# Twelve modulation units of a transformer kernel computed on TensorE instead of seven, five of them at changes between stages

## The chip, the cores and the metric

The kernel runs on one core of a Trainium2 chip. The metric is the device time of one execution in microseconds (us); the number given for a kernel is the median of its runs. TensorE is called PE in the rows (its weight loads PEld), VectorE is DVE, ScalarE is ACT, GpSimd is POOL, and SyncE, which issues the DMAs, is SP.

## The reference, cut to what matters

Two transformer blocks of two layers each run one after the other on 256 tokens of width 1024, in float32. The second block is modulated: each of its layers computes, from a condition vector, six rows of 1024 numbers (shift, scale and gate for the mixer, and the same for the feed-forward part), once for the latent tokens and once for 256 context tokens.

```python
for l in range(DEPTH):                               # second block, DEPTH = 2
    mod_l = jnp.split((silu(c) @ ada_w[l] + ada_b[l])[:, None, :], 6, axis=-1)
    mod_c = jnp.split((silu(c_ctx) @ ada_w[l] + ada_b[l])[None, None, :], 6, axis=-1)
    hl = modulate(x_lat, norm_g[l, 0], mod_l[0], mod_l[1])     # rms_norm * (1 + scale) + shift
    hc = modulate(x_ctx, norm_g[l, 0], mod_c[0], mod_c[1])
    ...                                              # even or odd mixer
    x_lat = x_lat + mod_l[2] * (mix_l @ w_out[l])
    x_lat = x_lat + mod_l[5] * conv_ffn(modulate(x_lat, norm_g[l, 1], mod_l[3], mod_l[4]), ...)
    ...                                              # the same for x_ctx with mod_c, in layer 0
```

The change concerns how `mod_l` and `mod_c` are computed and when. The first block does not use them.

## The kernel before

**Stages.** One program goes through the stages a0 (first attention mixer), f0 (its feed-forward part), a1, f1 (first block, layer 1), even (the even mixer of the second block), f2 (its feed-forward part), odd (the odd mixer) and f3. Each stage is a list of steps, a step being a list of weight keys and a function that emits instructions. `weave(a, b)` (L307) spreads the steps of b evenly between those of a.

**Weights.** All big matrices are streamed from HBM as units of up to 128 x 1056 numbers, in the order in which the steps name them. `fetch` (L481) issues the DMA of a unit into `raw` and splits it: ACT rounds it into `wh` (L496), DVE subtracts to get the rest `wl` (L497). Before a step that uses unit n is emitted, the units up to n + 4 are fetched (`UNITS_AHEAD`, L38). `raw`, `wh` and `wl` have four buffers each (L39 to L42), so unit n + 4 can only be split when unit n has been used up. A full product is three matmuls: high by high, high by low, low by high.

**Order.** The framework keeps the program order as a priority and orders each engine's instructions itself, taking the first whose inputs and buffers it expects to be free. The resulting order of each engine is fixed in the program.

**PSUM.** Accumulators come from pools: three banks `acc`, two `s`, two `t`, one `o` (L870). Output projections (`p_out`, L625), the gate half of a feed-forward part and the modulation units on PE all take an `acc` bank.

**Modulation.** The 6 x 1024 columns of one layer are 24 units of 256 columns; the two layers make units 0 to 47. `ada_upto` (L567) issues the units in order from a running counter `ada_at`. `ada(slot)` (L561) moves the counter on by the number that the table `ADA` (L317) holds for this slot. `ada_need(l, n)` moves it to where a coming stage needs it. There are two ways to compute a unit:
- on DVE: two blocks of 128 columns. Each loads 128 x 1024 numbers (`adaw`, 512 KB, from SP) and runs one multiply-and-reduce (L591) for each condition. Units 0 to 31 take two per block, units 32 to 47 one, as the context is not needed then.
- on PE (`p_ada`, L599), for the units in `ADA_PE` (L40): two weight units of 512 rows x 256 columns, which go through the `raw`, `wh`, `wl` ring like any other, 8 matmuls of 256 columns for each of them with the split condition `csil` as the stationary side, one copy to `adarow` on ACT (L616), four small matmuls that turn the rows, and one addition on DVE.

Before, `ADA_PE` is 13 to 19, and all seven lie in the middle of the even mixer (slots "e.0", "e.1", "e.2", with 3, 2 and 2 units), woven among the mLSTM heads' projections.

**Changes of stage.** `plan_attn0` and `plan_attn1` end with `p_out` of the last quarter of the mixer's rows, and the feed-forward part begins with gate and up products of `nh`, `nl`. The even mixer begins with `even_norm` (L1203): statistics, then `modulate` (L1134, per 128 channels one DVE `nt` L1143, one ACT `nh` L1145, one DVE `nl` L1146) over eight channel groups, interleaved with a scaling of x (L1216). f2 ends with the down products of the latents, while the context is already modulated for the odd mixer; the odd mixer's first products (`p_nout` of "kv" and "k", L531) are of the context.

Of the kernel before, what the change touches and what calls it, by code (L numbers as in the profile page):

```python
# [17 lines left out]
S = 256  # L18
# [18 lines left out]

UNITS_AHEAD = 4  # L38
RAW_BUFS = 4  # L39
ADA_PE = range(13, 20)  # L40
HI_BUFS = 4
LO_BUFS = 4  # L42
CUTS = 1
# [4 lines left out]
def _ar(a, n):  # L48
    return np.arange(a, a + n)
# [6 lines left out]
def unit_specs():  # L56
# [3 lines left out]
    def add(key, w, l, rows, cols):  # L60
        assert key not in u
        u[key] = (w, l, rows, cols)

    def halves(key, w, l, cols):
        for kh in range(2):
            add(key + (kh,), w, l, _ar(512 * kh, 512), cols)
# [11 lines left out]
                add(key + ("d", m, t), down, l, _ar(128 * j0, 128 * (j1 - j0)), _ar(128 * m, 128))  # L78

    for i in ADA_PE:  # L80
        halves(("ada", 0, i), "ada_w_2", 0, _ar(256 * i, 256))
    for g in range(2):
        for j, n in enumerate("qkv"):
            halves(("a", n, g), "hyb_w_in", 0, _ar(512 * j + 256 * g, 256))
# [222 lines left out]
def weave(a, b, tail=0):  # L307
    out, n, i = [], max(len(b) - tail, 0), 0
    for k, s in enumerate(a):
        out.append(s)  # L310
        while i < n and i * len(a) < (k + 1) * n:
            out.append(b[i])
            i += 1
    return out + b[i:]


ADA = {  # L317
    "a0.0": 0, "a0.1": 1, "a0.2": 1, "a0.3": 2, "f0": 1, "f1": 4, "e.0": 3, "e.1": 2, "e.2": 2, "f2": 28,
}


# [55 lines left out]
class Prog:  # L377
    def __init__(self):
        self.specs = unit_specs()
        self.ada_at = 0  # L380
        self.steps = self.plan()
        self.order = []
        seen = set()
        for keys, _ in self.steps:
            for k in keys:
                if k not in seen:
                    seen.add(k)
                    self.order.append(k)
        self.utab = unit_table(self.order, self.specs)
# [177 lines left out]
    def ada_upto(self, n, room=True):  # L567
# [3 lines left out]
        for i in range(a, self.ada_at):  # L571
            if i in ADA_PE:
                out += self.p_ada(i // 24, i % 24)
# [331 lines left out]
    def plan_attn0(self):  # L905
# [22 lines left out]
        def proj_a(g):  # L928
            b = boxes[g]
            return (self.p_rope(("a", "q", g), b, "q", -0.125) + self.p_rope(("a", "k", g), b, "k", None)  # L930
                    + self.p_v(("a", "v", g), b))
# [55 lines left out]
        out = self.p_open("0", first) + proj_a(0)  # L987
# [3 lines left out]
        out += weave(attend(boxes[3], "mask_c", 3, ext(1)),  # L991
                     self.ada("a0.3") + self.p_out(("o0", 0), 128, self.mixes(0, 6), S, self.x_add()))
        out += self.ada("a0.t")
        out += self.p_out(("o0", 1), 512, self.mixes(6, 8), S, self.x_add((self.st0,), "fn0"))
        return out + self.p_close()

    def plan_ffn1(self, l, st, nst, fill, gn=None, mid=(), side=()):
# [46 lines left out]
    def plan_attn1(self, st, fill, early):  # L1044
# [18 lines left out]
        def proj(g):  # L1063
            b = boxes[g]
            return (self.p_rope(("d", "q", g), b, "q", -0.125) + self.p_rope(("d", "k", g), b, "k", None)
                    + self.p_v(("d", "v", g), b))
# [51 lines left out]
        out = self.p_open("1", first) + fill + proj(0)  # L1118
# [1 line left out]
            out += weave(attend(g), proj(g + 1) + early("a1.%d" % g) + self.ada("a1.%d" % g))  # L1120
        out += weave(attend(3), early("a1.3") + self.ada("a1.3") + self.p_out(("o1", 0), 128, self.mixes(0, 6), S, self.x_add()))
        out += early("a1.t") + self.ada("a1.t")
        out += self.p_out(("o1", 1), 512, self.mixes(6, 8), S, self.x_add((self.st1,), "fn1"))
        return out + self.p_close()

    def scales(self, l, w):
# [136 lines left out]
    def plan_even(self, s1, s2):  # L1263
# [69 lines left out]
        def pairs(ts, i0, i1):  # L1333
            return Lazy(lambda: [(ts[i][0][:, p], ts[i][1][:, p]) for i in range(i0, i1) for p in range(2)])
# [201 lines left out]
        o_l = [self.p_out(("o2", "l%d" % i), 512, pairs(E.sl, i, i + 1), S, xm(LAT, *st[1:2 * i])) for i in range(2)]  # L1536
# [5 lines left out]
        def early(slot):  # L1542
            out = []
            for n, at in EC.items():
                if at == slot:
                    if n == "kvg":
                        out += [((), setup)] + kvg(0)
                    elif n == "g":
                        out += gprep(0)
                    elif n == "oc":  # L1550
                        out += self.ada_need(0, 12) + o_c
                    elif n[0] == "q":
                        out += proj_q(int(n[1]), False)
                    elif slot == "f1":
                        out += attend(int(n[1]), False)
            return out
# [7 lines left out]
        out = self.p_open("2", first) + early("e.a") + self.ada("e.a")  # L1564
# [25 lines left out]
        for k in slots:  # L1590
# [2 lines left out]
            out += weave(chain[k], fill[k], EV["tail"] if k in "b0123" else 0)  # L1593
            if k in "b012":
                out += decay(slots.index(k))
        out += o_l[1]
        yield out + self.p_close() + [((), lambda: self.evctx.close())] + self.plan_ffn2a(st[1])

    def plan_ffn2a(self, sl):
# [3 lines left out]
        out = self.p_open("f2")  # L1603
# [25 lines left out]
        for t, (j0, j1) in enumerate(THIRDS):  # L1629
# [8 lines left out]
            if t == 0:  # L1638
# [7 lines left out]
                n0 = len(out)  # L1646
# [20 lines left out]
                if i == 0:  # L1667
                    out.append(((), lambda: self.modulate(1, 0, st[0])))
        self.st_odd = st[1]
        return out[:n0] + weave(out[n0:], self.ada("f2")) + self.p_close()  # L1670

    def plan_ffn2b(self, st):
        l, key, W = 1, ("f3",), S + 2
# [224 lines left out]
```

## Time and profile before

| | us |
|---|---|
| median of 3 runs (lowest, highest) | 1726.1 (1724.31, 1729.87) |
| the profiled execution | 1726.9 |
| its span, first to last instruction | 1725.1 |
| PE busy in the span | 1670.7 (97%) |
| DVE busy | 1371.5 (80%) |
| ACT busy | 945.7 (55%) |

The profiled execution's own time is 1.8 us above its span and 0.8 us above the median. A matmul's recorded length overlaps its successor, so the distance from start to start tells what one costs in a stream. The granted clock of PE is given as a share of 2.4 GHz; the two levels are 2.4 and 1.2 GHz, and a value between them is a mean over the stretch.

### The profile page before, as it was taken

What the parts mean: (1) busy time and instruction counts of PE and PEld (TensorE: products, weight loads), DVE (VectorE), ACT (ScalarE), POOL (GpSimd) and SP (SyncE); (2) the same over time, 40 slices, a digit from 0 to 9 for tenths busy, and PEclk for the clock granted to TensorE, in tenths of its full rate; (3) what the DMA queues carried; (4) which work ended last, traced back from release to release, by engine and by line L of the source; (5) the groups of instructions that cost most, each with busy time, mean ns of one, the idle gap of its engine ahead of it and who ended that gap; (6) DMA issues with size and microseconds to landing.
All of it is one profiled execution on the core that took longest, in us unless ns stands there. A gap on an engine that the chain in (4) does not pass through costs nothing.

```text
span 1725.1 us, 31957 instructions
## 1 busy us (share of the span) xinstructions
PE 1670.7 (97%) x12336; PEld 1574.1 (91%) x12336; DVE 1371.5 (80%) x2830; ACT 945.7 (55%) x1687; POOL 59.0 (3%) x75
## 2 busy tenths in 40 slices
PE   7999999999899999999989999999998999999999
PEld 7999999999899999899978988888888998999999
DVE  6798999887787888766786888897779864479887
ACT  6666456656675768444545652342344554466554
POOL 0000000000100000100000000000000220000000
PEclk9999999999999999999989999999998999799999
DMA  8446776554456565334311555655549521135663
GB/s 305 140 142 220 231 219 210 173 173 132 125 173 194 184 206 162 123 124 133 110 62 41 181 182 165 189 169 185 181 150 315 184 62 38 62 121 165 198 191 123
DMA packets 80664, 277.97 MB, mean 161 GB/s; under 512 B 8960, under 2 KB 12160, under 8 KB 80256
## 3 DMA queue, kind: packets, MB, share of 16 engines
q1 hardware_dynamic: 79216, 273.30, 49.6%
q10 hardware_dynamic: 1296, 2.62, 0.4%
q8 instruction: 97, 1.59, 0.4%
q14 instruction: 55, 0.45, 0.1%
HBM read 274.84 MB, written 1.05 MB: 160 GB/s over the span
## 4 chain that ended last, share of the span: by engine, by line
PE 83%; DVE 10%; ACT 4%; issue 2%; DMA 0%; POOL 0%; DVEq 0%; ACTq 0%; POOLq 0%
PE acc L501 55%; PE s L501 20%; PE o L501 4%; DVE wl L497 3%; DVE junk L591 2%; PE ptp L820 2%; ACT wh L496 1%; PE tt L741 1%; DVE x L856 0%; DVE cc L1025 0%; PE stv L501 0%; PE tt L836 0%; DVE nt L1143 0%; ACT L1373 0%; DVE stq L691 0%
## 5 line engine op out<-in xcount | busy, mean ns | idle before, releaser
L496 ACT ACTIVATE wh<-raw 128x1024 fp32r<-128x1024 f32 (+4 forms) x446 | 453.7, 1025 | 453.5 <-PE acc L501 323.6
L497 DVE TENSOR_TENSOR wl<-raw,wh 128x1024 fp32r<-128x1024 f32 (+4 forms) x446 | 524.1, 1180 | 115.1 <-ACT wh L496 113.1
L501 PE MATMUL acc<-nh,wh 128*128 128x256 f32 (+2 forms) x872 | 269.0, 309 | 3.0 <-ACT nh L1145 1.9
L501 PE MATMUL acc<-nh,wl 128*128 128x256 f32 (+2 forms) x872 | 268.7, 308 | 0.5 <-DVE wl L497 0.3
L501 PE MATMUL acc<-nl,wh 128*128 128x256 f32 (+2 forms) x872 | 267.6, 308 | 0.0
L501 PE MATMUL acc<-wh,nh 128*128 128x256 f32 (+2 forms) x768 | 221.9, 290 | 12.4 <-ACT nh L642 7.9
L501 PE MATMUL acc<-wh,nl 128*128 128x256 f32 (+2 forms) x768 | 220.8, 290 | 6.2 <-DVE nl L1146 5.9
L501 PE MATMUL s<-nh,wh 128*128 128x256 f32 (+2 forms) x744 | 223.8, 301 | 2.1 <-ACT sm L1373 1.4
L501 PE MATMUL s<-nh,wl 128*128 128x256 f32 (+2 forms) x744 | 223.7, 301 | 0.0
L501 PE MATMUL s<-nl,wh 128*128 128x256 f32 (+2 forms) x744 | 223.4, 300 | 0.0
L501 PE MATMUL acc<-wl,nh 128*128 128x256 f32 (+2 forms) x768 | 220.8, 288 | 1.6 <-DVE wl L497 1.5
L501 PE MATMUL acc<-g,wh 128*128 128x256 f32 x1056 | 186.2, 279 | 2.7 <-ACT g L639 1.5
L501 PEld LDWEIGHTS acc<-nh,wh 128*128 128x128 f32 x872 | 165.3, 190 | 12.3 <-ACT nh L1145 2.1
L501 PEld LDWEIGHTS acc<-nh,wl 128*128 128x128 f32 x872 | 164.9, 189 | 9.5 <-DVE wl L497 1.2
L501 PEld LDWEIGHTS acc<-nl,wh 128*128 128x128 f32 x872 | 164.8, 189 | 8.6 <-DVE nl L1146 0.2
L591 DVE CUSTOM_DVE_ANT_0 junk<-adaw,sil,c0t 128x1024 f32<-128x1024 f32 x132 | 168.4, 1276 | 0.2
L501 PEld LDWEIGHTS acc<-g,wh 128*128 128x128 f32 x1056 | 160.0, 188 | 4.8 <-ACT g L639 1.9
L501 PEld LDWEIGHTS acc<-wh,nh 128*128 128x128 f32 x768 | 148.8, 194 | 14.7 <-ACT nh L642 8.2
L501 PEld LDWEIGHTS acc<-wh,nl 128*128 128x128 f32 x768 | 148.8, 194 | 8.8 <-DVE nl L1146 7.6
L501 PEld LDWEIGHTS acc<-wl,nh 128*128 128x128 f32 x768 | 148.5, 193 | 3.4 <-DVE wl L497 2.7
L501 PEld LDWEIGHTS s<-nh,wh 128*128 128x128 f32 x744 | 140.1, 188 | 8.4 <-ACT sm L1373 1.6
L501 PEld LDWEIGHTS s<-nl,wh 128*128 128x128 f32 x744 | 139.9, 188 | 6.0
(383 smaller groups left out, 3347.0 us busy)
## 6 DMA issues: line engine op xcount, KB each, us to landing
raw<-in_wts SPq DMA_DIRECT2D x342, 512.0 KB, 4.2
adaw<-in_ada SPq DMA_DIRECT2D x82, 512.0 KB, 4.3
raw<-in_wts SPq DMA_DIRECT2D x72, 448.0 KB, 3.4
raw<-in_wts SPq DMA_DIRECT2D x24, 384.0 KB, 3.2
x<-in_x SPq DMA_DIRECT2D x8, 256.0 KB, 7.1
raw<-in_wts SPq DMA_DIRECT2D x4, 408.0 KB, 3.8
rpb<-in_rpb ACTq DMA_DIRECT2D x1, 1536.0 KB, 6.6
raw<-in_wts SPq DMA_DIRECT2D x2, 528.0 KB, 3.6
```

Source lines behind the costliest of these rows:

```text
L496: nc.scalar.activation(hf[:, c], raw[:, c], AF.Copy)
L497: self.last_wl = nc.vector.tensor_sub(lf[:, c], raw[:, c], hf[:, c].bitcast(F32)).ins
L501: self.nc.tensor.matmul(o, a, b, start=start, stop=stop)
L591: self.nc.vector.tensor_tensor_reduce(out=junk, in0=tiles[j], in1=self.sil[:, c], scale=1.0, scalar=self.C["adab%d" % l][:, m:m + 1], op0= ...
L741: self.nc.tensor.transpose(ps[:, p, t * 128:(t + 1) * 128], src[:, t, p * 128:(p + 1) * 128], self.ident)
L820: self.nc.tensor.transpose(pt[:, kb], P[:, kb * 128:(kb + 1) * 128], self.ident)
```

## The change

`ADA_PE` becomes units 4, 9, 13 to 20, 46 and 47: twelve instead of seven. The keys of the weight units carry the layer, since 46 and 47 are units 22 and 23 of layer 1. The table gets slots at five changes of stage, and the counts move so that the counter still ends at 48:
- "a0.z", after the last `p_out` of a0: unit 4 (before: on DVE in f0)
- "a1.z", after the last `p_out` of a1: unit 9 (before: on DVE in f1)
- "e.a", after the context's output projection at the beginning of the even mixer: units 13 and 14 (before: in "e.0")
- "e.0", "e.1", "e.2": three, one and one units (15 to 19) instead of three, two and two
- "e.z", after the last output projection of the even mixer: unit 20 (before: on DVE in f2)
- "f2.z", after all steps of f2: units 46 and 47 (before: on DVE in f2)

f2 keeps 25 units on DVE (21 to 45) instead of 28 (20 to 47).

```diff
-ADA_PE = range(13, 20)
+ADA_PE = (4, 9, 13, 14, 15, 16, 17, 18, 19, 20, 46, 47)
...
     for i in ADA_PE:
-        halves(("ada", 0, i), "ada_w_2", 0, _ar(256 * i, 256))
+        halves(("ada", i // 24, i % 24), "ada_w_2", i // 24, _ar(256 * (i % 24), 256))
...
 ADA = {
-    "a0.0": 0, "a0.1": 1, "a0.2": 1, "a0.3": 2, "f0": 1, "f1": 4, "e.0": 3, "e.1": 2, "e.2": 2, "f2": 28,
+    "a0.0": 0, "a0.1": 1, "a0.2": 1, "a0.3": 2, "a0.z": 1, "f0": 1, "a1.z": 1, "f1": 3, "e.a": 2, "e.0": 3, "e.1": 1, "e.2": 1,
+    "e.z": 1, "f2": 25, "f2.z": 2,
 }
...
-        out += self.p_out(("o0", 1), 512, self.mixes(6, 8), S, self.x_add((self.st0,), "fn0"))
+        out += self.p_out(("o0", 1), 512, self.mixes(6, 8), S, self.x_add((self.st0,), "fn0")) + self.ada("a0.z")
...
-        out += self.p_out(("o1", 1), 512, self.mixes(6, 8), S, self.x_add((self.st1,), "fn1"))
+        out += self.p_out(("o1", 1), 512, self.mixes(6, 8), S, self.x_add((self.st1,), "fn1")) + self.ada("a1.z")
...
-        out += o_l[1]
+        out += o_l[1] + self.ada("e.z")
...
-        return out[:n0] + weave(out[n0:], self.ada("f2")) + self.p_close()
+        return out[:n0] + weave(out[n0:], self.ada("f2")) + self.ada("f2.z") + self.p_close()
```

The slot "e.a" was already called in `plan_even` and had no entry in the table.

## Rows read from the trace of the kernel before

**Rows 1.** The page: busy time by engine; the chain that ended last, by engine

```profile
PE 1670.7 (97%) x12336; PEld 1574.1 (91%) x12336; DVE 1371.5 (80%) x2830; ACT 945.7 (55%) x1687; POOL 59.0 (3%) x75
...
PE 83%; DVE 10%; ACT 4%; issue 2%; DMA 0%; POOL 0%; DVEq 0%; ACTq 0%; POOLq 0%
```

**Rows 2.** Busy time by stretch: stretch, length, busy us and count by engine, clock, DMA

```profile
136.00:143.00 7.00, 5.97 (x46) 5.26 (x46) 4.89 (x13) 3.25 (x8) 0.00 (x0) 1.00 0.66 224
466.00:474.00 8.00, 5.49 (x29) 4.76 (x28) 5.07 (x15) 4.34 (x13) 0.69 (x1) 0.79 0.43 129
698.00:714.00 16.00, 13.21 (x74) 11.95 (x73) 12.49 (x30) 6.51 (x12) 0.00 (x0) 0.79 0.28 88
938.00:950.00 12.00, 10.78 (x76) 10.30 (x76) 9.02 (x22) 5.68 (x12) 0.69 (x1) 0.86 0.14 44
1322.00:1342.00 20.00, 14.37 (x85) 13.25 (x84) 18.58 (x41) 6.87 (x14) 2.31 (x5) 0.74 0.65 212
1342.00:1352.00 10.00, 8.12 (x60) 7.13 (x58) 9.89 (x19) 7.54 (x15) 0.97 (x2) 1.00 0.84 301
714.00:868.00 154.00, 153.64 (x1072) 142.05 (x1071) 108.08 (x257) 78.02 (x165) 5.79 (x7) 1.00 0.39 125
984.00:1300.00 316.00, 315.79 (x1549) 263.63 (x1548) 256.39 (x386) 119.53 (x163) 0.00 (x0) 1.00 0.55 175
1300.00:1322.00 22.00, 22.00 (x195) 22.00 (x194) 22.00 (x38) 12.26 (x18) 1.54 (x1) 1.00 0.98 346
```

**Rows 3.** Timeline of PE: start, us, operation; a unit's first, 16th, turning matmuls, next

```profile
763.01 0.28 PE L501 MATMUL acc<-wh,csil 128*128 128x256 f32 x1
...
764.79 0.28 PE L501 MATMUL acc<-wl,csil 128*128 128x256 f32 x1
...
768.97 0.51 PE L501 MATMUL acc<-c0t,adarow 128*128 128x2 f32 x4
769.33 0.36 PE L501 MATMUL acc<-wl,csil 128*128 128x256 f32 x1
```

**Rows 4.** Groups by line and shape, DVE: count, busy us, mean ns, idle before

```profile
L497 DVE TENSOR_TENSOR wl<-raw,wh 128x1024 fp32r<-128x1024 f32 x342 | 415.9, 1219 | 96.2 <-ACT wh L496 94.9
L591 DVE CUSTOM_DVE_ANT_0 junk<-adaw,sil,c0t 128x1024 f32<-128x1024 f32 x132 | 168.4, 1276 | 0.2
```

**Rows 5.** Timeline of PE around the end of a0

```profile
136.14 0.37 PE L501 MATMUL acc<-mixl,wh 128*128 128x256 f32 x1
...
137.28 0.28 PE L501 MATMUL acc<-mixh,wl 128*128 128x256 f32 x1
...
138.83 0.44 PE L836 MATMUL tt<-c0t,on 128*128 128x128 f32 x2 [0.52 <-DVE on L832]
...
142.68 0.28 PE L501 MATMUL s<-nh,wh 128*128 128x256 f32 x1
...
160.65 0.39 PE L501 MATMUL acc<-nh,wh 128*128 128x256 f32 x1 [0.93 <-DVE gr L1022]
```

**Rows 6.** Timeline of PE: end of a1, beginning and end of the even mixer

```profile
465.57 0.37 PE L501 MATMUL acc<-mixh,wh 128*128 128x256 f32 x1
...
468.12 0.41 PE L1109 MATMUL tt<-c0t,on 128*128 128x128 f32 x2 [1.94 <-DVE on L1106]
...
701.09 0.40 PE L501 MATMUL acc<-wh,nh 128*128 128x272 f32 x1 [1.43 <-ACT nh L1145]
...
948.36 0.39 PE L501 MATMUL s<-nh,wh 128*128 128x256 f32 x1 [0.70 <-ACT wh L496]
```

**Rows 7.** Timeline of PE and DVE after the last product of f2

```profile
1325.10 0.39 PE L501 MATMUL acc<-wh,nh 128*128 128x256 f32 x1 [2.10 <-ACT nh L1145]
...
1326.42 1.21 DVE L497 TENSOR_TENSOR wl<-raw,wh 128x1024 fp32r<-128x1024 f32 x1
...
1328.42 0.58 PE L501 MATMUL acc<-wh,nl 128*128 128x256 f32 x1 [2.57 <-DVE nl L1146]
...
1339.01 1.27 DVE L591 CUSTOM_DVE_ANT_0 junk<-adaw,sil,c0t 128x1024 f32<-128x1024 f32 x1
```

## The prediction

> **What bounds the kernel now.** I read the page's busy times, then the chain that ended last, then the busy time by stretch, then the timeline of PE where a stretch falls short. PE is busy for 97% of the span and carries 83% of the chain [rows 1]. By stretch this splits in two. In the middle of the even mixer and in most of f2, PE is busy for 153.64 of 154 us and 315.79 of 316 us at the full clock [rows 2]: there every matmul added costs its whole time, and DVE work removed gives nothing, since DVE is not the limit. At the changes of stage PE falls short: it is idle for 1.03 us at the end of a0, 2.51 at the end of a1, 2.79 at the beginning of the even mixer, 1.22 at its end, 5.63 between f2 and odd (length less PE busy, 13.2 us in all) [rows 2]. In four of the five the granted clock is also below one, a mixture of 2.4 and 1.2 GHz, after waits such as those of 2.10 and 2.57 us [rows 2, 7]. One minus the clock times the length bounds what this costs: 1.7, 3.4, 1.7 and 5.2 us, 12.0 in all. So the change puts work where PE has at most 13.2 us of idleness, and 12.0 us that are lost to the lower clock. The question is how much of this the added work really reaches.
>
> **What a unit costs.** On PE: the 16 matmuls of a unit start 0.119 us apart ((764.79 - 763.01) / 15), 1.90 us, and its four turning matmuls take 0.36 us from the first to the next instruction [rows 3]: 2.26 us. Five more units are 11.3 us of PE. On DVE a unit gives back four reductions of 1.276 us (units 4, 9, 20) or two (46, 47), 16 in all or 20.4 us, and takes two splits of 1.219 us, ten in all or 12.2 us [rows 4]. So for units 46 and 47 DVE saves almost nothing: 2.55 us against 2.44 and one addition. ACT gets ten roundings and five row copies; 55% busy, it has room [rows 1]. The loads are even: ten 512 KB loads leave the modulation's queue entries and ten of the same size enter the weights', all from SP.
>
> **Place by place**, with what PE gets (+) and what a gap swallows (-):
>
> 1. Middle of the even mixer: two units fewer. PE is full there [rows 2], so -2 x 2.26 = -4.5. The bound is 0 if the heads' chains of DVE work then leave holes where the units filled; I take the full gain, as the row is as near to full as a row can be.
>
> 2. "e.a", +4.5. The stretch has 2.79 us of idleness [rows 2], the first of it a wait of 1.43 us for the modulated `nh` [rows 6]. A unit needs nothing that is modulated, so I let it swallow all of the idleness: +1.7. The bounds are +4.5 and, with the clock back as well, 4.5 - 2.8 - 3.4 = -1.7.
>
> 3. "a0.z", +2.3. At first sight it fits the wait ahead of 138.83. It does not: already at 136.14 to 137.28 PE has begun products of the last `p_out` with the half of the mixer that is ready (eight recorded matmuls, three to a column tile, so three tiles) [rows 5], and these hold all three `acc` banks. The unit comes later in program order and needs such a bank, so it can start only when most of the `p_out` is done, where PE is already taking up-products of f0 early (142.68) and is full. What it can still swallow is the wait of 0.93 us for the normalised rows at 160.65 [rows 5]: +1.4. Bounds: +2.3, and 2.3 - 1.0 - 0.9 = +0.4.
>
> 4. "a1.z", +2.3. The stage is built the same way, and the wait of 1.94 us at 468.12 [rows 6] again lies behind products of the last `p_out` that have begun (465.57). No wait follows that it could fill: +2.3. Bounds: +2.3, and 2.3 - 2.5 - 1.7 = -1.9 if it does get into the gap and the clock stays up.
>
> 5. "e.z", +2.3. PE waits 0.70 us for a weight split at 948.36 [rows 6]; the unit fills that: +1.6. Bounds: +2.3 and 2.3 - 1.2 - 1.7 = -0.6. The four reductions that unit 20 takes from f2 bring nothing, as PE is full there [rows 2].
>
> 6. "f2.z", +4.5. The waits of 2.10 and 2.57 us [rows 7] are 4.7 us, and the units are later only than products that are finished by then: swallowed. But the ring has four buffers. Before, the four splits ahead of the odd mixer are those of its first weights, the last at 1326.42 [rows 7]; after, they are those of units 46 and 47, and the odd mixer's first four come behind them, 4 x 1.22 = 4.9 us more on DVE before the latents are modulated. DVE is busy for 22.00 of 22 us ahead of the change and 18.58 of 20 and 9.89 of 10 us behind it, modulation reductions among it up to 1339.01 [rows 2, 7]. Against that, f2 has 51 modulation steps (50 blocks and a load) woven among 67 instead of 57; in the last 17, where DVE is full, these are 12.9 instead of 14.5, and with one reduction each DVE is relieved of 1.5 x 1.28 = 1.9 us. So the latents' modulation ends some 3.0 us later: +3.0. Bounds: +7.7 if the 4.7 us of waits come back behind late weights, and -5.2 if the splits find room and the clock stays up.
>
> Of what is queued there, the Trainium skill says, in "TensorE: Matmul & The Clock Gate", Part 2, that only weight loads are pulled ahead and matmuls stay in program order. By that a unit that waits for its split holds back all products behind it, which speaks against work at places where DVE is late. The rows agree in so far as PE starts nothing else in the 2.57 us before 1328.42 [rows 7].
>
> The sum: -4.5 + 1.7 + 1.4 + 2.3 + 1.6 + 3.0 = +5.5. On the profiled execution's 1726.9 us this is 1732.4; that execution is 0.8 us above the median of the runs, so I say 1732.
>
> **The rivals.**
>
> - *The clock stays up, faster.* The seven units at the changes (15.8 us) use up all 13.2 us of idleness, +2.6; the even mixer's middle gives -4.5; and with no long wait left PE keeps 2.4 GHz and half of the 12.0 us comes back, -6.0: -7.9, so 1719 (1713 with all of it). For it speaks that the lowered clock follows waits that a unit could fill [rows 2, 7]; against it the held banks at two places, and that at "e.a" and "f2.z" DVE, not PE, sets when the modulated inputs come. My sum has 9.1 of the 25.2 us lost there come back; this rival decides the sign from 5.5 us more, and makes the kernel measurably faster from 11.5 us more. The Trainium skill, in the same page's "Why this matters for your kernels", says that gaps between bursts of matmuls bring the half clock back. By that rule filling the waits is worth more than their length. The trace agrees that the clock is lower around waits, 0.74 from 1322 to 1342 [rows 2].
>
> - *The late weights cost nothing, no change.* The displaced splits slip into moments in which `modulate` waits for ACT, so "f2.z" costs 0 instead of 3.0 and "e.a" 0 instead of 1.7: +0.8, so 1727.7. For it: DVE is free for 3.5 of 16 us from 698 to 714 and 1.4 of 20 from 1322 to 1342 [rows 2]. Against it: that is less than the 4.9 us in the second place.
>
> - *The units do not land at the changes, slower.* The framework is free to put them where it expects room, and PE has none outside the gaps: all 11.3 us are added, 1738, and up to 2 us more where next weights are late. For it: 136.14 to 137.28 shows how freely later work is drawn forward [rows 5]. Against it: at "f2.z" and "e.a" little else is ready.
>
> **How the numbers follow.** The forecast's own case has 0.32 (1729.5 to 1735), no cost of late weights 0.28, the clock's recovery 0.26, no gap reached 0.14. Runs of this kernel can tell some 0.3% from no change, 5.2 us, so faster means under 1720.9 and slower over 1731.3. The forecast's case lies on both sides of the upper bound and gives 0.27 of its 0.32 to slower; the second rival gives 0.02 to slower; the third gives its whole 0.14; the first gives 0.25 to faster and 0.01 to the middle. So slower 0.43, same 0.32, faster 0.25. The range reaches from 1717, which leaves out the better part of the clock's case (0.1), to 1739, which leaves out the end of the last one (0.05 to 0.1): 1717 to 1739.
>
> **What would show it.** In any case: 192 matmuls with `csil` instead of 112, 48 with `adarow` instead of 28, 116 reductions instead of 132, 456 splits instead of 446, 72 loads of `adaw` instead of 82. Step 1 is right if the middle of the even mixer is some 4.5 us shorter with PE still full. Steps 3 and 4 are right if the matmuls of units 4 and 9 lie behind the waits for `on`, among the last `p_out` tiles or the first f0 and f1 products, and these waits are as long as before; wrong if the waits are gone. Step 6 is right if units 46 and 47 follow the last f2 product without a gap, the first split for "kv" then ends later than 1327.6 after the same start, and PE waits for it or for `nl`; wrong if PE is continuous from the end of f2 and its clock stays at one. The prediction as a whole falls if the granted clock at the changes rises to one: then the first rival has won.

## The result, and the profile after

The changed kernel takes 1741.7 us (median of 6 runs, 1738.33 to 1742.89) against 1725.07 for the kernel before beside it: a ratio of 1.0093, interval 1.0076 to 1.0110. A second set of six gave 1739.9 and 1.0084 [1.0065, 1.0103]. So it is slower by some 15 us; the forecast was 1732 with 1739 as the upper end. The profiled execution, 1738.33 us with a span of 1736.5, is the fastest of its set, so its trace shows only 11.4 us more than that of before (1736.5 less 1725.1). The difference to 15 us is taken up below with the clock.

The page: busy time and the chain that ended last, which answer to [rows 1]; then, from the operations on the tiles `csil` and `adarow` and from the groups by shape, the counts (lines after L317 are one further down than before):

```profile
PE 1679.0 (97%) x12436; PEld 1583.3 (91%) x12436; DVE 1367.6 (79%) x2813; ACT 962.3 (55%) x1706; POOL 58.9 (3%) x75
...
PE 81%; DVE 11%; ACT 4%; issue 3%; POOL 1%; DMA 0%; DVEq 0%; ACTq 0%; POOLq 0%; SPq 0%
```

```profile
L502 PE MATMUL acc<-wh,csil x96: 275/281/388, 145.1 to 1335.2; 128*128 128x256 f32 x96
...
L502 PE MATMUL acc<-wl,csil x96: 276/281/386, 145.2 to 1335.3; 128*128 128x256 f32 x96
...
L502 PE MATMUL acc<-c0t,adarow x48: 165/251/374, 152.1 to 1340.6; 128*128 128x2 f32 x48
```

```profile
L592 DVE CUSTOM_DVE_ANT_0 junk<-adaw,sil,c0t 128x1024 f32<-128x1024 f32 x116 | 148.6, 1281 | 0.2
```

The change does what it says: 192 products with `csil`, 48 turning matmuls, 116 reductions. PE is as full as before and has 100 more matmuls.

Busy time by stretch, as in [rows 2] (stretch, length, busy us and count of PE, weight loads, DVE, ACT, POOL, then clock, DMA share and GB/s), each window moved by the delay and made longer where units were added:

```profile
136.00:147.00 11.00, 9.95 (x80) 9.26 (x80) 8.92 (x21) 7.26 (x16) 0.00 (x0) 1.00 0.46 150
467.00:480.00 13.00, 9.87 (x65) 9.15 (x64) 9.44 (x22) 8.96 (x22) 1.21 (x2) 0.87 0.40 132
...
721.00:868.00 147.00, 146.72 (x1022) 135.12 (x1021) 101.15 (x244) 71.43 (x153) 4.45 (x7) 1.00 0.36 115
868.00:900.00 32.00, 21.50 (x106) 17.61 (x105) 25.67 (x87) 11.72 (x34) 4.04 (x3) 0.79 0.11 35
942.00:957.00 15.00, 13.84 (x113) 12.91 (x111) 11.53 (x26) 9.87 (x19) 0.70 (x1) 1.00 0.15 43
991.00:1307.00 316.00, 315.78 (x1549) 263.39 (x1548) 250.41 (x373) 121.21 (x165) 0.00 (x0) 1.00 0.53 168
...
1329.00:1349.00 20.00, 13.96 (x86) 12.75 (x86) 20.00 (x40) 10.08 (x19) 0.14 (x1) 0.80 0.73 253
1349.00:1359.00 10.00, 10.00 (x78) 10.00 (x78) 7.81 (x17) 6.18 (x13) 2.18 (x5) 0.88 0.53 183
```

```profile
698.00:721.00 23.00, 19.97 (x142) 18.20 (x141) 20.02 (x44) 11.61 (x18) 3.12 (x4) 1.00 0.54 183
```

Length less PE busy gives the idle time that the units were to fill: 1.05 us at the end of a0 (before 1.03), 3.13 at a1 (2.51), 3.03 at the even mixer's beginning (2.79), 1.16 at its end (1.22), 6.04 between f2 and odd with nothing in the ten us behind (5.63 and 1.88). So the units went to the changes of stage and the holes are nearly all still there; only behind f2 did they close by some 1.5 us. The wait of 0.70 us for a split that the unit at the even mixer's end was to fill is still there too, as long as before, just behind that window (957.66, waiting for `wl`). At the beginning and the end of the even mixer the clock is one in this execution (before 0.79 and 0.86), but the beginning became some 6 us longer all the same (below). In the second trace of the changed kernel, after_again, the end of the even mixer has 0.89:

```profile
942.00:957.00 15.00, 14.25 (x105) 13.77 (x105) 11.39 (x26) 9.27 (x19) 0.69 (x1) 0.89 0.13 40
```

### The profile page after: what moved, and what is told of

The parts are those of the page before. It is cut to its first block, busy times and chain, and to the rows that moved or that the text cites. A ratio compares the mean times of both kernels' runs of the same rounds, so it can differ in the third digit from the quotient of the medians.

```text
span 1736.5 us, 32193 instructions
## 1 busy us (share of the span) xinstructions
PE 1679.0 (97%) x12436; PEld 1583.3 (91%) x12436; DVE 1367.6 (79%) x2813; ACT 962.3 (55%) x1706; POOL 58.9 (3%) x75
## 3 DMA queue, kind: packets, MB, share of 16 engines
HBM read 274.84 MB, written 1.05 MB: 159 GB/s over the span
## 4 chain that ended last, share of the span: by engine, by line
PE 81%; DVE 11%; ACT 4%; issue 3%; POOL 1%; DMA 0%; DVEq 0%; ACTq 0%; POOLq 0%; SPq 0%
PE acc L502 53%; PE s L502 20%; PE o L502 4%; DVE wl L498 3%; PE ptp L821 2%; DVE junk L592 2%; ACT wh L497 1%; DVE nt L1144 1%; PE tt L742 1%; DVE x L857 1%; ACT L1028 0%; DVE stq L692 0%; DVE nl L1147 0%; PE stv L502 0%; PE tt L837 0%
## 5 line engine op out<-in xcount | busy, mean ns | idle before, releaser
L497 ACT ACTIVATE wh<-raw 128x1024 fp32r<-128x1024 f32 (+3 forms) x456 | 464.3, 1026 | 435.6 <-PE acc L502 308.8
L498 DVE TENSOR_TENSOR wl<-raw,wh 128x1024 fp32r<-128x1024 f32 (+3 forms) x456 | 537.8, 1184 | 113.9 <-ACT wh L497 111.6
L592 DVE CUSTOM_DVE_ANT_0 junk<-adaw,sil,c0t 128x1024 f32<-128x1024 f32 x116 | 148.6, 1281 | 0.2
L502 PEld LDWEIGHTS s<-nh,wl 128*128 128x128 f32 x744 | 139.9, 188 | 6.6 <-DVE wl L498 0.5
```

What stands on the lines that cost most here:

```text
L497: nc.scalar.activation(hf[:, c], raw[:, c], AF.Copy)
L498: self.last_wl = nc.vector.tensor_sub(lf[:, c], raw[:, c], hf[:, c].bitcast(F32)).ins
L502: self.nc.tensor.matmul(o, a, b, start=start, stop=stop)
L592: self.nc.vector.tensor_tensor_reduce(out=junk, in0=tiles[j], in1=self.sil[:, c], scale=1.0, scalar=self.C["adab%d" % l][:, m:m + 1], op0= ...
```

## The experiments

**How they are compared.** 138 runs of the kernel before, beside the experiments, lie between 1718.0 and 1732.4 us, and most of that is the granted clock of the execution, 0.976 to 0.988: a straight line through them falls by 1.12 us for each 0.001 of clock and leaves 1.25 us of scatter. So two numbers are given for each kernel: the difference of the means, and the same with the difference in clock taken out at that price ("at equal clock", good to about 1 us for the parts of the change; one unit in o2_one shows 4.5 where its matmuls are 2.26, and that was not explained). The second number takes the clock out whether the change moved it or not, so it says what the work costs, and the first says what the kernel takes. The six runs of before beside the changed kernel have no clock on record; its second number is counted from the line. Expectations written early quote the slope from the first 35 runs, 1.26 us.

| kernel | median (runs) | mean less before's | mean clock (before 0.982) | at equal clock | ratio, interval |
|---|---|---|---|---|---|
| changed kernel | 1741.7 (6) | +16.1 | 0.9792 | +12.7 | 1.0093 [1.0076, 1.0110] |
| the same again | 1739.9 (6) | +14.2 | 0.9802 | +12.0 | 1.0084 [1.0065, 1.0103] |
| even_move | 1728.1 (11) | +3.1 | 0.9833 | +4.5 | 1.0019 [1.0008, 1.0031] |
| even_skip | 1726.5 (11) | +0.3 | 0.9821 | +0.3 | 1.0003 [0.9989, 1.0016] |
| mid_more | 1731.4 (12) | +5.6 | 0.9818 | +5.2 | 1.0032 [1.0016, 1.0048] |
| e3_fill | 1734.8 (7) | +9.2 | 0.9796 | +6.6 | 1.0060 [1.0039, 1.0081] |
| ez_only | 1724.8 (12) | +0.8 | 0.9842 | +3.0 | 1.0005 [0.9989, 1.0021] |
| az_only | 1724.4 (12) | -0.8 | 0.9858 | +3.3 | 0.9995 [0.9978, 1.0013] |
| az_sbank | 1724.5 (12) | -0.9 | 0.9839 | +1.0 | 0.9996 [0.9981, 1.0012] |
| f2z_only | 1729.7 (12) | +4.1 | 0.9804 | +2.3 | 1.0020 [1.0010, 1.0031] |
| f2z_nosplit | 1725.7 (12) | -0.8 | 0.9833 | +0.8 | 0.9998 [0.9980, 1.0017] |
| f2_skip | 1724.9 (12) | 0.0 | 0.9827 | +1.1 | 1.0001 [0.9988, 1.0014] |
| no_em | 1733.2 (12) | +7.6 | 0.9830 | +8.9 | 1.0045 [1.0029, 1.0061] |
| em_ez | 1733.4 (7) | +7.2 | 0.9810 | +6.4 | 1.0046 [1.0029, 1.0063] |
| after_o3 | 1740.7 (6) | +14.0 | 0.9815 | +13.8 | 1.0085 [1.0057, 1.0113] |
| o3_pe | 1722.0 (12) | -4.1 | 0.9889 | +3.8 | 0.9981 [0.9965, 0.9997] |
| o3_four | 1727.3 (12) | +1.9 | 0.9886 | +9.6 | 1.0013 [0.9997, 1.0029] |
| o3_one | 1730.3 (9) | +5.8 | 0.9802 | +4.1 | 1.0036 [1.0020, 1.0053] |
| o2_one | 1731.3 (12) | +6.0 | 0.9804 | +4.5 | 1.0035 [1.0022, 1.0048] |

The edits below are against the kernel before, with the new calls of `ada` and the longer key from the change in all of them.

### The even mixer: what are two units worth in its middle?

even_move:

```diff
-"e.0": 3, "e.1": 2, "e.2": 2
+"e.a": 2, "e.0": 3, "e.1": 1, "e.2": 1
```

> Only the even mixer is changed: units 13 and 14 go to its opening ("e.a"), three, one and one units stay in its middle; the seven units on TensorE are the same, so no work is added. Theory 1 (TensorE pays for what it gets, and the two units taken from the middle leave holes at 870 to 895 where the heads' chains are then exposed): the mixer gives back only part, and the kernel becomes 1 to 3 us slower, with the delay against the kernel before rising by 7 to 12 us up to 740 us and falling to 1 or less at 850 before it rises again. Rival A, the prediction's steps 1 and 2 (-4.5 in the middle, +1.7 at the opening): 2.8 us faster. Rival B (the opening swallows nothing and also delays the modulated inputs): more than 4 us slower.

even_skip (the rows of the two units are set to zero, which is not shown):

```diff
-            if i in ADA_PE:
+            if i in (17, 19):
+                continue
+            if i in ADA_PE:
```

> Units 17 and 19 of the even mixer's middle are not computed at all (their rows of the modulation are left at zero), everything else stands as before. It measures what two units fewer in the middle are worth by themselves. The prediction's step 1 (TensorE is full there): 4.5 us faster, two times 2.26. Theory 1 (part of it comes back as holes at 870 to 895, where TensorE waits for the heads' chains on VectorE and ScalarE): 0 to 2.5 us faster, with TensorE's idle time from 868 to 895 longer by 2 us or more than before.

mid_more:

```diff
-ADA_PE = range(13, 20)
+ADA_PE = (13, 14, 15, 16, 17, 18, 19, 20, 21)
-"e.1": 2, "e.2": 2, "f2": 28
+"e.1": 3, "e.2": 3, "f2": 26
```

> Units 20 and 21 go to TensorE in the middle of the even mixer, which then has nine units (three in each of the slots "e.0", "e.1", "e.2") instead of seven; f2 keeps 26 units on VectorE. Two units fewer there were worth nothing. Theory 2 (the end of the middle is set by the heads' chains as much as by TensorE, with holes of some 6 us at 870 to 895): 0 to 3 us slower at equal clock, as the added matmuls fill a part of the holes. The prediction's step 1 read the other way (TensorE is full there): 4.5 us slower.

Two units fewer gain nothing (+0.3); two more cost 5.2 at equal clock. The middle lies at a knee: PE is full up to 868, and yet something else ends the stretch just as late. Busy time by stretch, the kernel before and then even_skip:

```profile
840.00:868.00 28.00, 27.64 (x192) 25.44 (x191) 23.29 (x64) 12.82 (x30) 2.56 (x2) 1.00 0.44 142
868.00:900.00 32.00, 25.98 (x126) 21.09 (x126) 28.36 (x89) 12.86 (x35) 2.69 (x3) 0.84 0.15 49
```

```profile
840.00:868.00 28.00, 26.41 (x186) 24.32 (x184) 22.88 (x58) 12.67 (x29) 2.64 (x2) 1.00 0.35 116
868.00:900.00 32.00, 22.70 (x115) 18.72 (x116) 26.40 (x91) 12.59 (x35) 2.61 (x2) 0.84 0.08 25
```

PE's idle time in these 60 us goes from 6.38 to 10.89 us: the 4.51 us that the two units leave come back as idle time to the hundredth (2 x 2.26 = 4.52). The waits of PE in 868 to 900, before and then even_skip (waiter, released by, total us, times, longest), name the heads' chain on DVE, `hs` and `W`:

```profile
PE ht L1520 <- DVE hs L1519: 2.2, 1, 2.2
```

```profile
PE ht L1523 <- DVE hs L1522: 3.9, 1, 3.9
PE s L502 <- DVE W L1487: 2.6, 1, 2.6
```

The changed kernel, which also has two units fewer there, has the same waits in 868 to 900 (PE 21.50 of 32 us, above):

```profile
PE ht L1521 <- DVE hs L1520: 3.9, 1, 3.9
PE s L502 <- DVE W L1485: 2.6, 1, 2.6
```

That it is this chain that ends the stretch is read from the waits; no run made the chain shorter. With nothing gained in the middle, the 4.5 us of even_move at equal clock are those of the two units at the opening, their whole price (3.1 us in the mean).

What they do at the opening is seen in the changed kernel, in PE's timeline and in DVE's:

```profile
701.17 0.65 PE L706 MATMUL bc<-c0t,rs 128*128 128x128 f32 x4 [2.08 <-POOL rs L662]
...
704.64 0.28 PE L502 MATMUL acc<-wh,csil 128*128 128x256 f32 x1
...
712.53 0.39 PE L502 MATMUL acc<-wh,nh 128*128 128x272 f32 x1 [0.71 <-DVE mods L622]
```

```profile
710.37 1.01 DVE L498 TENSOR_TENSOR wl<-raw,wh 128x816 fp32r<-128x816 f32 x1
...
718.35 0.89 DVE L1147 SCALAR_TENSOR_TENSOR nl<-nt,mods,nh 128x256 fp32r<-128x256 f32 x2
```

The units run from 704.64, behind the wait for the statistics and not in it. Their splits, the next stage's and the row additions `mods` stand among the steps of `modulate`, whose last `nl` ends at 719.24; before it ended at 709.79 (start 708.92, 0.87 us), and some 3 us of delay came from a0 and a1. So modulation is some 6 us later.

e3_fill was to put the two units to use beside the exposed chain:

```diff
-"e.2": 2
+"e.2": 0, "e.3": 2
```

> Nothing but a move within the even mixer: the two units of slot "e.2" go to "e.3", so that they stand beside the last chains of the heads at 870 to 895, where TensorE idles for 6 us and its clock is 0.83. Theory 1 (TensorE's 4.5 us in the middle are not what ends it, since two units fewer gave nothing): the idle time from 868 to 900 falls by 2 us or more, and the kernel is the same or up to 3 us faster by the clock. Rival (the two weights and splits beside the chains delay them on VectorE): 1 to 4 us slower.

It fails, by more than its rival said: +6.6 at equal clock, +9.2 in the mean. The longest wait for `hs` is 3.8 us instead of 2.2, PE's idle time from 868 to 900 is 8.12 us instead of 6.02, and the clock there 0.69 instead of 0.84. The units don't fill the chain's waits but lengthen them; DVE is busy for only 20.60 of these 32 us, so it isn't the splits' bare amount, and which step holds the chain was not followed further.

### The other places, one at a time

ez_only, az_only, f2z_only:

```diff
+ADA_PE = range(13, 21)                        # ez_only
+"e.z": 1, "f2": 27
...
+ADA_PE = (4, 9, 13, 14, 15, 16, 17, 18, 19)   # az_only
+"a0.z": 1, "a1.z": 1, "f1": 3
...
+ADA_PE = (13, 14, 15, 16, 17, 18, 19, 46, 47) # f2z_only
+"f2": 26, "f2.z": 2
```

> Only unit 20 goes to TensorE, after the even mixer's last output projection ("e.z"); f2 keeps 27 units on VectorE. Theory 2 (its matmuls are paid, and what lies around it is not shortened): 2 to 3 us slower at equal clock. The prediction's step 5: 1.6 us. The clock's rival: the clock near 940 rises from 0.83 to one and the kernel is up to 0.6 us faster.

> Only units 4 and 9 go to TensorE, at the ends of a0 and a1; f1 keeps three units on VectorE. Theory 1 (the units come behind the wait for the normalisation and swallow little of it): 2 to 4 us slower, 0.5 to 1.5 of it at a0 and 1.5 to 2.5 at a1, with the waits of about 2 us in front of the normalisation's matmul as long as before. Rival (the stages' gaps are reached after all, or the clock comes back): 0 or faster.

> Only units 46 and 47 go to TensorE, at the end of f2 ("f2.z"); f2 keeps 26 units on VectorE. Theory 1 (the displaced splits of the odd mixer's first weights cost, as in the whole change, where the delay rose by 4.0 us): 3 to 5 us slower. The prediction's step 6: 3.0 us slower. Rival, late weights cost nothing: 0. Rival, the clock comes back: 3 to 5 us faster.

At equal clock they cost 3.0, 3.3 and 2.3; the prediction had 1.6, 3.7 and 3.0. In the means az_only and ez_only differ from before by no more than their intervals allow, since their executions had a higher clock (0.9858 and 0.9842); f2z_only had a lower one.

az_sbank asks why units 4 and 9 don't reach the gap:

```diff
-                    box.ps = self.acc()
+                    box.ps = self.s_tile() if i in (4, 9) else self.acc()
```

> Units 4 and 9 go to TensorE at the ends of a0 and a1, as in the run of these alone, but their accumulator is one of the two banks of the pool s, which the last output projection doesn't use. Prediction, step 3 (the three banks of acc, held by begun tiles, keep the units out of the gap): the units' matmuls now lie in the waits of about 2 us ahead of the normalisation's matmul, these waits shrink by 1 us or more each, and the kernel is 1 to 3 us faster than with the acc bank at equal clock, so 1 to 2.5 us slower than before instead of 3.6. Rival (it is the program's order or the weights' splits that keep them out): the same 3 to 4 us and the same waits as with the acc bank.

It was the bank that kept them out. In the changed kernel unit 9 lies behind the wait for `on` and the `p_out` tiles, and unit 4 likewise (145.09, behind a wait of 0.52 us at 139.08 that is as long as before); with a bank of the pool s both run ahead of it. PE's timeline in the changed kernel, then in az_sbank:

```profile
469.27 0.41 PE L1110 MATMUL tt<-c0t,on 128*128 128x128 f32 x2 [1.95 <-DVE on L1107]
...
477.43 0.38 PE L502 MATMUL acc<-wh,csil 128*128 128x256 f32 x1 [0.62 <-DVE x L843]
```

```profile
465.36 0.36 PE L501 MATMUL s<-wh,csil 128*128 128x256 f32 x1
...
470.41 0.61 PE L501 MATMUL s<-c0t,adarow 128*128 128x2 f32 x4 [1.30 <-ACT adarow L616]
471.82 0.41 PE L1109 MATMUL tt<-c0t,on 128*128 128x128 f32 x2 [0.81 <-DVE mods L621]
```

The two units cost 1.0 instead of 3.3 at equal clock; in the means the two kernels do not differ (-0.9 and -0.8). At a1 the wait of 1.95 us is gone, but the unit brings two of its own, 1.30 us for the row copy and 0.81 for the addition, which now stand in front of the normalisation. At a0 the wait for `on` is 0.65 us, so at neither place did the idle time shrink by the 1 us that was expected.

f2z_nosplit asks what costs at the end of f2:

```diff
+                if key[:2] != ("ada", 1):
                     self.last_wl = nc.vector.tensor_sub(lf[:, c], raw[:, c], hf[:, c].bitcast(F32)).ins
-            self.W[key] = (h, l)
+            self.W[key] = (h, h if key[:2] == ("ada", 1) else l)
```

> Units 46 and 47 at the end of f2 as in the run of these alone, but their weights are not split: the low part is not made, and the matmuls that would read it read the rounded part again. This leaves out the low part of these two units and nothing else; TensorE's work is the same, and VectorE is spared four splits, 4 x 1.22 = 4.9 us. The prediction's step 6 (TensorE's work is swallowed, the four displaced splits are what costs): the 2.8 us at equal clock fall to 0 or below. Rival (it is TensorE's 4.5 us that cost, as at the other places): 2 us or more remain.

With the same matmuls and four splits fewer the two units cost 0.8 at equal clock instead of 2.3, and -0.8 instead of +4.1 in the mean. So most of the price is the splits' and not PE's, as step 6 had it; that it falls to 0 or below at equal clock was a little too much, as far as numbers good to about 1 us can tell. PE's timeline of the changed kernel shows the places:

```profile
1334.05 0.61 PE L502 MATMUL acc<-c0t,adarow 128*128 128x2 f32 x4 [1.09 <-ACT adarow L617]
...
1338.59 0.58 PE L502 MATMUL acc<-wh,nh 128*128 128x256 f32 x1 [2.99 <-ACT nh L1146]
1339.96 1.02 PE L502 MATMUL acc<-c0t,adarow 128*128 128x2 f32 x4 [0.58 <-ACT adarow L617]
```

The waits of [rows 7] are not gone but have others in their place, while DVE is busy for 20.00 of 20 us (1329 to 1349).

### Do the parts add up?

> The changed kernel itself once more, with the granted clock of every run. Over 35 runs of the kernel before, time falls by 1.26 us for each 0.001 that the granted clock is higher (0.979 to 0.987, 1730 to 1718 us). Theory 2: the change costs 12 to 14 us at equal clock (the parts measured alone: 4.9 for the even mixer, 2.8 for f2's end, 3.6 for a0 and a1, and some 2 for "e.z"), and what the median has beyond that is the clock; median 1738 to 1742 with a clock of 0.978 to 0.981, and runs at 0.982 near 1739. Rival (the parts interact, for instance through the order of the whole program): at equal clock 16 us or more over the kernel before.

no_em (the change without "e.a", middle 3, 2, 2):

> The change without its part in the even mixer's opening: units 4, 9, 20, 46 and 47 go to TensorE at the other four places, the middle keeps its seven units (three, two and two). Theory 2 (parts add up at equal clock): 3.6 + 3.0 + 2.8 = 9.4, so 9 to 10 us slower than before at equal clock, and 3 to 5 us faster than the whole change; with the clock of the parts (0.982 to 0.986) the median lies at 1732 to 1736. Rival (the whole has a lower clock because its places influence each other): the clock is 0.980 or lower here too, and the median 1737 or more.

em_ez ("e.a": 2, "e.1": 1, "e.2": 1, "e.z": 1 and "f2": 27 alone):

> The two parts of the change that lie in the even mixer together and nothing else: units 13 and 14 at its opening, one and one in the slots "e.1" and "e.2", unit 20 at its end. Alone the first costs 3.1 us in the mean at a clock of 0.9833, the second 0.2 at 0.9842. Theory 2 with independent parts: 3 to 4 us slower, clock 0.983 or higher. If the missing 3 to 4 us of the whole change come from these two meeting: 6 us or more slower, at a clock of 0.981 or lower.

At equal clock they do: 4.5 + 3.0 + 3.3 + 2.3 = 13.1 against 12.0 and 12.7 for the whole; 3.0 + 3.3 + 2.3 = 8.6 against 8.9 for no_em; 4.5 + 3.0 = 7.5 against 6.4 for em_ez. In the means they don't: 7.2 against some 15, 4.1 against 7.6, 3.9 against 7.2. The clock is what doesn't add: three of the four parts raise it by themselves, by 0.0012 to 0.0037, and put together they lose it again (0.980 for the whole).

The traces of before and of the changed kernel, laid side by side, say where the 11.4 us between these two executions arise. One and the same instruction starts later in the changed kernel:

| instruction | before | changed | later by |
|---|---|---|---|
| ahead of the even mixer's opening (ACT `exh`) | 688.38 | 691.71 | 3.33 |
| near the end of the even mixer (ACT `sm`) | 924.85 | 929.76 | 4.91 |
| behind "e.z" (DVE `uu`) | 967.31 | 974.14 | 6.83 |
| end of f2 (DVE `rv`) | 1319.38 | 1326.30 | 6.92 |
| in the odd mixer (DVE `rec`) | 1506.09 | 1516.99 | 10.90 |

So a0 and a1 cost 3.3, the opening and the middle of the even mixer together 1.6, "e.z" 1.9 and "f2.z" 4.0, where the prediction had 3.7, -2.8, 1.6 and 3.0. Of the 5.9 us between 11.4 and the forecast sum of 5.5, the even mixer's opening and middle make 4.4, although the clock at the opening was the higher one in the changed kernel's trace.

### Where the clock goes, and a kernel that is faster than both

In most profiles (not in those of o3_pe, o3_four and az_only) the largest loss of clock is not at the places of the change but in the odd mixer. The kernel before, busy time by stretch and PE's timeline:

```profile
1450.00:1460.00 10.00, 7.65 (x56) 6.38 (x55) 4.77 (x12) 4.07 (x10) 1.64 (x1) 1.00 0.14 41
1460.00:1470.00 10.00, 10.00 (x46) 8.89 (x45) 3.53 (x9) 3.71 (x8) 0.00 (x0) 0.51 0.00 0
1470.00:1480.00 10.00, 10.00 (x44) 8.88 (x43) 4.10 (x11) 2.73 (x6) 0.00 (x0) 0.50 0.01 2
1480.00:1490.00 10.00, 9.48 (x67) 9.12 (x67) 2.43 (x7) 5.90 (x13) 0.00 (x0) 0.79 0.00 0
```

```profile
1459.03 0.66 PE L820 MATMUL ptp<-c0t,sm 128*128 128x128 f32 x4 [1.44 <-ACT sm L1804]
```

After a wait of 1.44 us PE runs at 1.2 GHz for some 25 us, busy all the time: half clock looks like a full engine on the page. How long this lasts differs between executions even where nothing was changed in the odd mixer. In az_only's profile, the one with the highest clock (0.992), a wait of 1.79 us stands at the same place (1453.86), and the clock behind it falls much less:

```profile
1460.00:1470.00 10.00, 9.79 (x65) 8.82 (x65) 5.77 (x16) 3.90 (x8) 0.00 (x0) 0.84 0.00 0
1470.00:1480.00 10.00, 9.48 (x72) 9.12 (x71) 2.39 (x7) 6.09 (x13) 0.00 (x0) 0.86 0.01 2
```

o3_pe puts units 46 and 47 there; o3_four takes 44 to 47, o3_one 47 alone, o2_one puts 47 one attention group earlier, f2_skip leaves 46 and 47 out, after_o3 is the whole change with "o.3" for "f2.z":

```diff
-"f2": 28
+"f2": 26, "o.3": 2
```

> Units 46 and 47 go to TensorE within the odd mixer's last attention group (slot "o.3"), at about 1455 to 1465, where TensorE waits 1.44 us and then runs at half clock for some 25 us in nearly every profile; f2 keeps 26 units on VectorE. If the clock there follows how full TensorE is: the clock comes back earlier, 4.5 us of added matmuls stand against up to 12 us lost there, and the kernel is 2 to 6 us faster. If the clock doesn't follow: 4.5 us slower, or up to 9 if the units themselves run at half clock.

> Units 46 and 47 are not computed at all (their rows of the modulation stay zero), f2 keeps 26 units on VectorE, and nothing is put into the odd mixer. It separates what f2 gains when it is rid of them from what the odd mixer gains when they fill it. If the 4 us of the run with the two units in the odd mixer come from f2's relief: 4 us or more faster here too. If they come from the clock in the odd mixer, which the added matmuls bring back: within 2 us of the kernel before, at its clock of 0.981 to 0.983, and half clock from 1460 to 1490.

> Units 44 to 47 go to TensorE within the odd mixer's last attention group, twice as many as in the run with 46 and 47 there; f2 keeps 24 units on VectorE. If two units bring the clock back already, two more only cost: 4.5 us more than with two, so within 2 us of the kernel before, at a clock of 0.989 or higher. Rival (the clock there still has something to give, the two gave back 8 of some 12 us): 0 to 2 us more than with two.

> One unit (47) instead of two goes to TensorE within the odd mixer's last attention group; unit 46 stays on VectorE in f2. If one unit also keeps TensorE out of the wait of 1.4 us ahead of the long stretch at half clock: the clock is 0.988 or higher as with two, and 2.3 us less of matmuls make it 5 to 7 us faster than before. If it takes two to do that: the clock stays at 0.982 to 0.985 and the time within 3 us of the kernel before.

> The same one unit (47), but in the attention group before (slot "o.2"), where TensorE is full at the full clock. If what counts is the place, the wait of 1.4 us at about 1459 with the half clock behind it: it stays, and the unit costs its 2.3 us at a clock of 0.981 to 0.983. If any change of the order around there brings the clock back: 0.986 or higher, and a gain.

> The whole change, but units 46 and 47 in the odd mixer's last attention group instead of at the end of f2. Alone, the two cost 4 us at the end of f2 and gain 4 us in the odd mixer. If the parts add up: 8 us faster than the changed kernel, 1731 to 1734, with the clock at 0.985 to 0.988. If the whole's low clock has another place: it stays below 0.983 and the time above 1735.

o3_pe is the one version that beats both kernels: 1722.0 us, 0.9981 [0.9965, 0.9997], clock 0.987 to 0.991 in all twelve runs. At equal clock it costs 3.8, so what it wins is clock. f2_skip shows that ridding f2 of the two units is worth 0.0, so the 4.1 us are the odd mixer's. The traces agree: counted from before's trace, o3_pe is 3.2 us ahead in front of this place (a DVE `mixl` ends at 1452.44 and not at 1455.62) and 7.0 us ahead behind it (a DVE `x`, 1486.03 and 1493.06), f2_skip 3.3 and 2.5. Busy time by stretch of o3_pe, and a unit in PE's timeline:

```profile
1450.00:1460.00 10.00, 8.47 (x57) 7.85 (x54) 7.77 (x16) 6.78 (x14) 1.64 (x1) 0.85 0.50 158
1460.00:1470.00 10.00, 10.00 (x75) 8.69 (x74) 6.42 (x17) 5.04 (x12) 0.00 (x0) 0.98 0.28 80
1470.00:1480.00 10.00, 9.85 (x80) 8.82 (x79) 3.25 (x10) 5.99 (x13) 0.00 (x0) 1.00 0.00 0
```

```profile
1456.28 0.38 PE L501 MATMUL acc<-wh,csil 128*128 128x256 f32 x1 [1.20 <-DVE mods L621]
...
1458.89 0.41 PE L501 MATMUL acc<-wh,csil 128*128 128x256 f32 x1
```

The clock falls here too (the products with `csil`, 0.28 us long at full clock, are 0.41 long up to 1458.89), but the second unit's matmuls stand where the wait of 1.44 us for `sm` was, and by about 1460 the clock is back. o3_four pays 6.0 us for two units more at the same clock: what was to be had was had. In o3_one and after_o3 the units did not land there: the framework drew them forward, to 1447.29 and to 1455.62 to 1462.8, ahead of the same wait. o3_one and o2_one (1443.95) even turned out to be one program: their traces hold the same instructions in the same order on PE, DVE and ACT, so the +5.8 and the +6.0 are one measurement made twice. o3_one, and then after_o3, by stretch and with that wait:

```profile
1460.00:1470.00 10.00, 10.00 (x45) 8.56 (x43) 3.53 (x9) 3.48 (x9) 0.00 (x0) 0.50 0.00 0
```

```profile
1459.54 1.12 PE L820 MATMUL ptp<-c0t,sm 128*128 128x128 f32 x4 [1.78 <-ACT sm L1804]
```

```profile
1470.00:1480.00 10.00, 9.76 (x44) 8.71 (x44) 3.60 (x11) 4.18 (x11) 0.00 (x0) 0.54 0.00 0
1480.00:1490.00 10.00, 10.00 (x44) 9.00 (x42) 3.44 (x10) 3.22 (x7) 0.00 (x0) 0.50 0.00 0
```

```profile
1470.24 0.65 PE L820 MATMUL ptp<-c0t,sm 128*128 128x128 f32 x4 [1.45 <-ACT sm L1804]
```

So the expectations of o3_one and after_o3 fell on the placing: the slot in the table is not the place on the engine. For o2_one the wait stayed (1.78 us), as its first alternative had it, but the unit cost more than 2.3 us. The Trainium skill says in "TensorE: Matmul & The Clock Gate", "Why this matters for your kernels", that idle gaps between bursts bring the half clock back. The trace agrees in that 0.51 and 0.50 stand behind 1.44 us of idleness, a shorter gap than the page speaks of. Whether in o3_pe it is the dense matmuls behind the wait or the changed wait itself (1.20 instead of 1.44 us) was not told apart.

## Why the prediction was wrong, by its own steps

The sign was right, the size was not: +5.5 predicted, 12.0 and 12.7 measured at equal clock, and the clock added some 2 to 3 more.

1. *Middle of even, -4.5.* **This is the step that failed.** even_skip measures it: +0.3, with 4.51 us more of idle time where 4.52 us of matmuls were taken away. I read "PE full for 153.64 of 154 us" [rows 2] as "PE is the bound", and named the case in which it isn't (the heads' chains leave holes) as a bound, with no weight in any rival. The stretch behind, 868 to 900, with PE busy for 25.98 of 32 us and DVE for 28.36, would have shown that PE waits there for the heads' chain as it is; I had left it out of the rows.
2. *"e.a", +1.7.* 4.2 (4.5 of even_move less 0.3), near the upper bound of +4.5. In the mean, with the clock that even_move had, it is 2.8 (3.1 less 0.3). The units came after the wait that they were to fill, and their four splits and two additions went into the modulation.
3. *"a0.z" and "a1.z", +3.7.* 3.3. The reason was right too: az_sbank shows the banks. The wait of 0.93 us that was to be swallowed at a0 is 0.39 us in the changed kernel (162.99).
4. *"e.z", +1.6.* 3.0. The unit filled nothing: the wait of 0.70 us for a split stands behind it as it stood before. With that wait PE's idle time there is 1.86 us (1.16 + 0.70) as against 1.22, so the place costs the unit's 2.26 us and 0.64 more.
5. *"f2.z", +3.0.* 2.3 by f2z_only at equal clock, 4.0 between the two traces, and the splits are most of it.

Of the 6.5 to 7.2 us that are missing at equal clock, steps 1 and 2 make 4.8 and 2.5, "e.z" 1.4; the rest goes the other way. Two slips in the working change nothing: the 9.1 us that my sum has come back are 8.9 (2.8 + 0.9 + 0.7 + 4.5), and the times of the rivals were counted from 1726.9 without the 0.8 us that the forecast takes off.

Of the rivals, "late weights cost nothing" is out (f2z_nosplit). "The units do not land at the changes" came nearest in time, 1738 to 1740, but not in its mechanism: they did land near the changes, and the gaps stayed. "The clock stays up" is not borne out: in the changed kernel's first trace the clock at two of the places is one, but the time there did not fall, and the clock of the whole execution became lower. Nor is that rise shown to be the units' doing. At the end of the even mixer the second trace has 0.89. At the opening, o3_one and o2_one, one program that leaves the opening as it was, have 0.79 in one execution and 1.00 in the other:

```profile
698.00:714.00 16.00, 13.21 (x67) 11.70 (x67) 12.87 (x30) 7.81 (x14) 0.00 (x0) 0.79 0.27 89
```

```profile
698.00:714.00 16.00, 13.21 (x81) 11.55 (x80) 15.05 (x35) 9.13 (x17) 0.00 (x0) 1.00 0.32 103
```

What no step of mine held is that the clock of one execution is decided mainly elsewhere, in stretches that the change does not touch, and differs between executions of one program by up to 0.012.

What stays open: why the parts raise the clock when they stand alone and lose it together. The odd mixer is where most of it is lost, but the changed kernel's profile has 0.50 there like that of before, and per-stretch clocks are known for one execution of each kernel only, for two of the changed one and of o3_one.

## What to carry to other kernels

A stretch in which an engine is full is not proof that this engine ends it: look at the stretch behind, and take the work away once, before counting its removal as a gain. Work moved into a gap must be able to start before the gap (bank, weights, inputs), and it brings its own copies, splits and additions to engines that are late there. Compare two versions at equal clock as well as by their medians, and look for stretches in which a busy engine runs at half clock.

## What the runs showed of the hardware that I had not expected

Executions of one program differ by 14 us (1718.0 to 1732.4) with the granted clock, 1.12 us for each 0.001. One program had a granted clock of 0.79 in one execution and of 1.00 in another in the same stretch (698 to 714). Behind a wait of 1.44 to 1.79 us in the odd mixer PE ran at 1.2 GHz for as little as 10 us (az_only) and as much as 37 us (o3_one), in a stretch with many short matmuls (64 rows or 64 columns) in which it was busy for nearly all of the time. 4.5 us of added matmuls, half of them where that wait had been, made the kernel 4.1 us faster.
